# The first norm of the last block: factors applied to sums, gain rows spread by TensorE, and an early half of the second gate products

## The chip, the cores and the metric

The kernel runs as one program on one core of a Trainium2 chip. The metric is device time in microseconds (us) of one execution. TensorE (PE, with its weight loads shown as PEld), VectorE (DVE), ScalarE (ACT), GpSimd (POOL) and SyncE (SP) each have their own instruction stream; instructions of one engine run in order, and engines wait for each other at semaphores. Transfers from memory are issued by SP and POOL here.

## The reference, cut to what matters

A first block of mixers and a routed expert layer is followed by a norm, and that by two layers of a second block, which begins with a norm and a gated feed-forward part. The change sits where the two blocks meet. What is computed there, for 256 tokens of width 1024 in 32-bit floats:

```python
for e in range(32):                                   # two of the 32 experts count for a token
    h = silu(x2d @ w_gate[e]) * (x2d @ w_up[e])       # 1024 -> 256
    y = y + combine[:, e:e + 1] * (h @ w_down[e])     # 256 -> 1024
h = h + y
x = rmsnorm(h, final_norm_g)                          # ends the first block
# second block, layer 0
xn = rms_norm(x, ffn1_norm_2[0])
x = x + 0.5 * (silu(xn @ w_gate) * (xn @ w_up)) @ w_down
```

Both norms divide each token by its root mean square and multiply by a row of gains. So the normed token is its raw sum, times both rows of gains, times one number for the token: the token's factor.

## The kernel before, in words

The 256 tokens are two halves of 128 (j = 0, 1), the 1024 channels two halves of 512 (n = 0, 1). `Moe.run` goes through the experts in eight quads of four (q = 0 to 7); the tokens of an expert, at most 32, stand on 32 partitions of the quad's 128. For each quad:

- `up(a, q, 0)` and `up(a, q, 1)`, L1236: the gate products and the up products, 32 each for the two, `mx<-mw,XG` in the trace (eight blocks of channels by four experts; each half is 32 instructions that the trace may show as two records each, so that a quad has 128);
- `act`, L1403: the message `msg` from silu and the slot weights (ACT, DVE), transposed on TensorE, copied as `mhT` (ACT);
- `down(q, hT)`, L1246: 16 products `mx<-mw,mhT` of 512 columns, the two channel halves in two tiles of their own;
- `back(q, ys, n)`, L1268: each half is cut into a high part (`yh`, ACT) and a low part (`yl`, DVE), which go back to the tokens by products with the one-hot matrix, `acc<-yh,OHT` and `acc<-yl,OHT`, onto the running sums `py[j, n]`. For quad 7's second half the two parts are called `yr`.

Between them other work of the routing is laid: in quad 0, after `down`, the second part of the slot weights (`acc<-cw,OH`, `acc<-mask,ones`), `beyond`, and one of the sums' starts (`acc<-x,ident`); in each quad the gathering of the next quad's tokens. The order on each engine is the program's where `K.ordered` is set; elsewhere a scheduler places instructions.

Weights come through a ring of slots `mw` in SBUF by `load_next`, all issued on SyncE in a fixed order, each when the slot it needs has been read for the last time. `spare(name, slot)` uses a slot of the ring for another tile: the row `fg` of the first norm's gains, for which POOL issues a transfer that repeats the row on all 128 partitions (L1329), and a scratch tile for squares. The second norm's row is `grow`, spread in the same way by `K.gain_row` (L197). `par` are small parameters of later layers, laid out by transposes (L125, L1474) and a product with ones (`mx<-par,ones`) in quad 7.

After quad 7 the norm of the first block and the next one are joined: `gained` multiplies the sums by `fg` (DVE), `square` and `square_x` give the sums of squares before and after the gains (ACT), and a list of one-column steps (`eps`, then `nra`, `nri`, `nrc`) gives each half's factor `rs[j]` (DVE). `Block2.first_part`, L1596, then makes the normed tokens (`norm`: `xn<-x,nri,grow` on DVE, eight transposes), and the first weights of the feed-forward part meet them. Half j = 0 is multiplied whole (`whole(i)`: `acc<-wr,x`, in 32-bit floats, 8 products of 512 columns); half j = 1 and all later work by high and low parts of tokens (`X`) and weights (`wh` on ACT, `wl` on DVE), three products for one (`mm`: `acc<-wh,X`, `acc<-wl,X`, 24 products). From then on the feed-forward part's own loop (`ffn`, L1694) runs: `acc<-X,wh` and `acc<-X,wl` on L246. `unit()` takes the next piece of weights and so also places its `wh` and `wl`.

## Time and profile before

| | us |
|---|---|
| median of 3 runs | 1619.53 (1617.61 to 1621.09) |
| the profiled execution | 1621.05 |
| its span | 1619.4 |
| PE busy in the span | 1548.0 (96%) |
| DVE busy | 1033.5 (64%) |
| ACT busy | 826.9 (51%) |
| POOL busy | 38.8 (2%) |

The profile is of one execution, so its durations add up to 1621.05 us, of which 1.65 lie around the span. A row of the timeline says when an instruction, or a run of like ones (x32), started, how long it took, on which engine and source line, what it wrote and read, and in brackets how long the engine had been idle before it and what ended that. A line such as L48 or L246 is that of a helper that many places call, so one goes by the names of the tiles. The expert stage runs from about 240 to 437 us; the join of the blocks lies between 423 and 461 us; everything after is the second block.

### The profile page before, as it was taken

The numbers are of one execution on the slowest core, as the hardware profiler recorded it, in microseconds if no ns is written. First come the engines' busy times: TensorE is split into PE (matmuls) and PEld (weight loads), VectorE is DVE, ScalarE is ACT, GpSimd is POOL, SyncE is SP. The second block draws the span as 40 slices with busy tenths as digits, with TensorE's granted clock in tenths as the row PEclk, the third lists the DMA queues.
The fourth block names the chain that finished last, engine by engine and source line by source line (L and its number), as shares of the span: only waits on it lengthen the run. The fifth ranks groups of instructions, "written<-read, shape, count | busy, mean of one in ns | idle before, by whom it ended". The sixth has DMA issues, their size and how long they took to land.

```text
span 1619.4 us, 25065 instructions
## 1 busy us (share of the span) xinstructions
PE 1548.0 (96%) x9718; PEld 1279.3 (79%) x9718; DVE 1033.5 (64%) x1913; ACT 826.9 (51%) x1406; POOL 38.8 (2%) x132
## 2 busy tenths in 40 slices
PE   8999998887799999999999999999999999999998
PEld 6989864443378888889878888888888989778887
DVE  6766651111376656868986665666658779876653
ACT  5633421111356544668645654455546677455643
POOL 3000000001000000000000000000000000000000
PEclk9999998999899999999999999999999999999999
DMA  6431599999966656553456655656565534455653
GB/s 201 146 101 66 214 383 395 420 420 418 350 195 185 193 183 193 171 166 98 154 182 197 195 193 182 195 183 192 176 211 187 157 124 153 167 159 186 199 177 112
DMA packets 195644, 331.29 MB, mean 205 GB/s; under 512 B 11972, under 2 KB 150674, under 8 KB 183362
## 3 DMA queue, kind: packets, MB, share of 16 engines
q1 hardware_dynamic: 186208, 315.19, 56.6%
q0 software_dynamic: 4528, 13.41, 2.5%
q8 instruction: 77, 1.26, 0.3%
q10 hardware_dynamic: 4786, 1.05, 0.3%
q14 instruction: 45, 0.37, 0.1%
HBM read 328.25 MB, written 1.38 MB: 204 GB/s over the span
## 4 chain that ended last, share of the span: by engine, by line
PE 70%; DMA 6%; DVE 3%; ACT 2%; issue 1%; ACTq 0%; SPq 0%; DVEq 0%
PE acc L246 40%; PE mx L246 19%; PE acc L48 8%; PE mx L48 3%; DMA mw<-in_exp_w_down 3%; DMA mw<-in_exp_w_up 2%; DMA mw<-in_exp_w_gate 1%; DVE wl L258 1%; DVE wl L48 1%; PE mx L1976 0%; PE mx L2000 0%; ACT fsq L48 0%; ACT wh L277 0%; ACT p L1991 0%; PE mx L2046 0%
## 5 line engine op out<-in xcount | busy, mean ns | idle before, releaser
L258 DVE TENSOR_TENSOR wl<-wr,wh 128x1024 fp32r<-128x1024 f32 x358 | 436.6, 1223 | 269.6 <-ACT wh L277 267.0
L277 ACT ACTIVATE wh<-wr 128x1024 fp32r<-128x1024 f32 x358 | 377.9, 1058 | 365.6 <-PE acc L246 256.7
L246 PE MATMUL acc<-X,wh 128*128 128x256 f32 (+1 forms) x1664 | 357.1, 329 | 0.0
L246 PEld LDWEIGHTS acc<-X,wh 128*128 128x128 f32 x1664 | 277.2, 191 | 25.2 <-issue 4.2
L246 PE MATMUL acc<-X,wl 128*128 128x256 f32 x1152 | 237.2, 285 | 0.0
L246 PEld LDWEIGHTS acc<-X,wl 128*128 128x128 f32 x1152 | 186.4, 191 | 6.9
L246 PE MATMUL mx<-X,wh 128*128 128x512 f32 x640 | 162.0, 393 | 0.0
L246 PEld LDWEIGHTS mx<-X,wh 128*128 128x128 f32 x640 | 114.6, 189 | 19.8
L246 PE MATMUL acc<-wh,hh 128*128 128x512 f32 x288 | 112.2, 390 | 0.0
L246 PE MATMUL acc<-wl,hh 128*128 128x512 f32 x288 | 112.2, 390 | 0.0
L246 PE MATMUL acc<-wh,hl 128*128 128x512 f32 x288 | 112.2, 389 | 0.0
L246 PEld LDWEIGHTS mx<-X,wl 128*128 128x128 f32 x640 | 88.4, 190 | 7.0
L246 PE MATMUL mx<-X,wl 128*128 128x256 f32 x640 | 90.5, 282 | 0.0
L48 PE MATMUL mx<-mw,XG 128*32 128x256 f32 x1024 | 66.3, 403 | 8.0 <-DMA mw<-in_exp_w_up 6.0
L48 PEld LDWEIGHTS mx<-mw,XG 128*32 128x32 f32 x1024 | 34.9, 116 | 37.4 <-issue 9.1
L246 PEld LDWEIGHTS acc<-wh,hl 128*128 128x128 f32 x288 | 54.1, 188 | 11.2
L246 PEld LDWEIGHTS acc<-wl,hh 128*128 128x128 f32 x288 | 54.1, 188 | 11.1
L246 PEld LDWEIGHTS acc<-wh,hh 128*128 128x128 f32 x288 | 54.1, 188 | 11.1
L246 PE MATMUL acc<-wh,m 128*128 128x512 f32 x192 | 61.3, 394 | 0.0
L48 DVE COPY xr<-mx 128x512 f32<-128x512 f32 x8 | 5.5, 691 | 72.7 <-ACT xr L48 72.7
L246 PE MATMUL acc<-xh,wh 128*128 128x256 f32 x176 | 50.4, 286 | 0.0
L246 PE MATMUL acc<-xh,wl 128*128 128x256 f32 x176 | 50.0, 284 | 0.0
(640 smaller groups left out, 2518.7 us busy)
## 6 DMA issues: line engine op xcount, KB each, us to landing
wr<-in_w_in SPq DMA_DIRECT2D x44, 1024.0 KB, 5.4
wr<-in_ffn_w_gate SPq DMA_DIRECT2D x88, 512.0 KB, 4.0
wr<-in_ffn_w_up SPq DMA_DIRECT2D x88, 512.0 KB, 5.0
wr<-in_ffn_w_down SPq DMA_DIRECT2D x40, 1024.0 KB, 5.0
mw<-in_exp_w_gate SPq DMA_DIRECT2D x32, 1024.0 KB, 15.1
mw<-in_exp_w_up SPq DMA_DIRECT2D x32, 1024.0 KB, 16.8
mw<-in_exp_w_down SPq DMA_DIRECT2D x31, 1024.0 KB, 17.9
wr<-in_w_out SPq DMA_DIRECT2D x20, 1024.0 KB, 4.9
```

Of the source, the lines that this page charges most:

```text
L48: return lambda *a, **k: self.tc.keep_in_program_order(f(*a, **k))
L246: self.engines()[2].matmul(out, l, r, start=start, stop=stop, skip_group_check=share)
L258: i = self.K.engines()[0].tensor_sub(l, v, h)
L277: self.K.engines()[1].activation(h, v[:, q:q + c], AF.Copy)
```

## The change

`down` writes both channel halves into one tile of two banks, and `back` reads them from it. The first half of quad 1's products (`up(a, 1, 0)`) is called in quad 0 right after `down`, ahead of the slot weights, and its `load_next` with it. The two rows of gains come as single rows of 4 KB, onto two partitions of one tile, and a new function `every` spreads each with two products of ones (`mx<-fg,ones`) and two copies on ACT; the first is called after `up(a, 7, 1)`, the second after quad 7's parameter steps, and a product of both rows (`both`) is made. For the first half of tokens, `turn` multiplies the sums by `both`, `turned` transposes the result right away, and `whole` runs on tokens without their factor. The factor comes in twice: `act` in `ffn` scales the first gate and up sums by it, and before the tokens are cut into high and low parts, `x0` is multiplied by the factors, spread over the partitions by a product of a diagonal (`dg`) with ones (`pr`). The squares and steps of the second half of tokens come first, those of the first half after it.

```diff
         def down(q, hT):
-            ys = []
+            y = K.mx.tile([P, 2, 512], F32, name="mx")
             for n in range(2):
-                y = K.mx.tile([P, 512], F32, name="mx")
...
+        def every(out, i):
+            b = K.mx.tile([P, 2, 512], F32, name="mx")
+            for n in range(2):
+                K.mm(b[:, n], K.ones[32 * i:32 * i + 1], rows_[i][:, 512 * n:512 * n + 512])
+            V, S, _ = K.engines()
+            for n in range(2):
+                S.activation(out[:, 512 * n:512 * n + 512], b[:, n], AF.Copy)
...
+            order = [(v, j) for v in (yh, yl) for j in range(2)]
+            if q == 7 and n:
+                order.sort(key=lambda o: o[1])
...
+            if q != 1:
+                a = K.mx.tile([P, 1024], F32, name="mx")
+                up(a, q, 0)
+                load_next(4)
+            if q == 7:
+                fg = spare("fg", 12, n=2048)
+                rows_ = [fg[32 * i:32 * i + 1, D:] for i in range(2)]
+                for i, src in enumerate((A["final_norm_g"], A["ffn1_norm_2"][0])):
+                    nc.gpsimd.dma_start(rows_[i], bass.AP(tensor=src.tensor, offset=src.offset, ap=[[0, 1], [1, D]]))
+                fg = fg[:, :D]
+            up(a, q, 1)
             load_next(4)
             if q == 7:
-                fg = spare("fg", 11)
-                src = A["final_norm_g"]
-                nc.gpsimd.dma_start(fg, bass.AP(tensor=src.tensor, offset=src.offset, ap=[[0, P], [1, D]]))
-            up(a, q, 1)
-            load_next(4)
+                every(fg, 0)
...
             if q == 7 and B:
                 next(par, None)
+                B.given = K.xp.tile([P, D], F32, name="grow")
+                every(B.given, 1)
+                both = spare("both", 13)
+                K.V.tensor_mul(both, fg, B.given)
             y = down(q, hT)
             load_next(4)
             if q == 0:
+                a = K.mx.tile([P, 1024], F32, name="mx")
+                up(a, 1, 0)
+                load_next(4)
                 slot_weights(1, 8)
...
+        def turn(n):
+            V.tensor_mul(x0[:, half[n]], py[0, n], both[:, half[n]])
+        def turned(n):
+            pt.append(K.mx.tile([P, 4, P], F32, name="mx"))
+            for k in range(4):
+                K.T.transpose(pt[n][:, k], x0[:, (4 * n + k) * P:(4 * n + k + 1) * P], K.ident)
+        back(7, y, 1)
+        turn(0)
         gained(0, 0)
-        back(7, y, 1)
...
+        turn(1)
+        turned(0)
+        turned(1)
+        square(0, 0, sq)
+        square(1, 0, sq)
+        for j, n in ((1, 0), (1, 1), (0, 1)):
+            gained(j, n)
...
# Block2.first_part
+        for k4, p in zip(k4s, pt):
+            S.activation(x0[:, k4], p, AF.Copy)
+        square(1, 1, fsq)
+        for n in range(2):
+            square_x(1, n, fsq)
         unit()
         whole(0)
+        run(es[1])
+        next(norm)
...
+        square(0, 1, fsq)
+        for n in range(2):
+            square_x(0, n, fsq)
         unit()
         whole(3)
+        next(norm)
+        run(es[0])
         self.stream.ahead = AHEAD
-        self.mm(1, us)
-        for k0 in range(0, KD, 4):
-            self.parts(0, slice(k0, k0 + 4), x0[:, k0:k0 + 4])
+        dg = pool.tile([P, P], F32, name="dg", tag="hl")
+        V.tensor_scalar(dg, K.ident, rs[0], None, op0=OP.mult)
+        self.mm(1, us[:2])
+        pr = K.mx.tile([P, P], F32, name="mx")
+        K.mm(pr, K.ones, dg)
+        for k4 in k4s:
+            V.tensor_mul(x0[:, k4], x0[:, k4], pr[:, None].to_broadcast([P, 4, P]))
+            self.parts(0, k4, x0[:, k4])
+        self.mm(1, us[2:])
```

TensorE in quad 0, from its down products to quad 1's; `XG_2524` and `XG_2525` are quad 1's gathered tokens, `cw` the combine weights. Before:

```order
L48 MATMUL mx<-mw,mhT 32x512 x16
L48 MATMUL acc<-cw,OH_2276 128x5 x7
L48 MATMUL acc<-cw,OH_2277 128x5 x7
L48 MATMUL acc<-mask,ones 128x32 x2
L48 MATMUL acc<-x,ident 128x512
L48 MATMUL acc<-yh,OHT 128x512 x2
```

After the change, TensorE at the same place:

```order
L48 MATMUL mx<-mw,mhT 32x512 x16
L48 MATMUL mx<-mw,XG_2524 32x256 x16
L48 MATMUL mx<-mw,XG_2525 32x256 x16
L48 MATMUL acc<-cw,OH_2276 128x5 x7
L48 MATMUL acc<-cw,OH_2277 128x5 x7
L48 MATMUL acc<-mask,ones 128x32 x2
```

The first 32 of quad 1's 64 gate and up products moved ahead of the slot weights and of quad 0's `back`.

TensorE in quad 7, up to its down products; `XG_3634` and `XG_3635` (after: `XG_3628`, `XG_3629`) are its tokens. Before:

```order
L48 MATMUL mx<-mw,XG_3634 32x256
L125 MATMUL mx<-ident,par 128x120
L125 MATMUL mx<-ident,par 128x86
L48 MATMUL mx<-mw,XG_3634 32x256
L48 MATMUL mx<-par,ones 128x512
L48 MATMUL mx<-par,ones 128x32
L1474 MATMUL mx<-ident,par 128x2
L48 MATMUL mx<-mw,XG_3634 32x256 x14
L48 MATMUL mx<-mw,XG_3635 32x256 x16
L48 MATMUL mx<-mw,XG_3634 32x256 x16
L48 MATMUL mx<-mw,XG_3635 32x256 x16
L48 MATMUL mx<-ident,msg 128x128 x2
```

After the change, TensorE from the last up products of quad 7 on:

```order
L48 MATMUL mx<-mw,XG_3629 32x256 x16
L48 MATMUL mx<-fg,ones 128x512 x2
L125 MATMUL mx<-ident,par 128x120
L125 MATMUL mx<-ident,par 128x86
L48 MATMUL mx<-ident,msg 128x128 x2
L48 MATMUL mx<-par,ones 128x512
L48 MATMUL mx<-par,ones 128x32
L1507 MATMUL mx<-ident,par 128x2
L48 MATMUL mx<-fg,ones 128x512 x2
L48 MATMUL mx<-mw,mhT 32x512 x16
```

The parameter products moved from among the gate products to between the last up product and `down`, and the rows' products stand with them.

DVE from the norm products of the second half of tokens to the low parts of its transposed tokens. Before:

```order
L48 SCALAR_TENSOR_TENSOR xn<-x,nri,grow 128x512 x2
L48 TENSOR_TENSOR wl<-wr,wh 128x1024
L48 TENSOR_TENSOR X<-mx,X 128x4x128 x2
L48 TENSOR_TENSOR wl<-wr,wh 128x1024
L48 TENSOR_TENSOR X<-x_3884,X 128x4x128 x2
```

After the change, DVE at the same place, followed by the first of the other half's one-column steps:

```order
L48 SCALAR_TENSOR_TENSOR xn<-x,nri,grow 128x512 x2
L48 TENSOR_TENSOR wl<-wr,wh 128x1024 x3
L48 TENSOR_TENSOR X<-mx,X 128x4x128 x2
L48 TENSOR_SCALAR rse<-fst 128x1
L48 SCALAR_TENSOR_TENSOR fa<-fst,rse 128x1
```

Three low parts of weights in place of one now stand ahead of the tokens' low parts, and the first of the four stands ahead of the second half's own one-column steps.

## Rows read from the trace of the kernel before

**Rows 1.** The page's part 4: the chain that ended last, by engine, by line

```profile
PE 70%; DMA 6%; DVE 3%; ACT 2%; issue 1%; ACTq 0%; SPq 0%; DVEq 0%
PE acc L246 40%; PE mx L246 19%; PE acc L48 8%; PE mx L48 3%; DMA mw<-in_exp_w_down 3%; DMA mw<-in_exp_w_up 2%; DMA mw<-in_exp_w_gate 1%; DVE wl L258 1%; DVE wl L48 1%; PE mx L1976 0%; PE mx L2000 0%; ACT fsq L48 0%; ACT wh L277 0%; ACT p L1991 0%; PE mx L2046 0%
```

**Rows 2.** Windows; busy us by engine, then granted clock, DMA share, GB/s

```profile
270.00:272.00 2.00, 2.00 (x44) 1.23 (x40) 0.00 (x0) 0.00 (x0) 0.00 (x0) 1.00 0.23 90
272.00:274.00 2.00, 2.00 (x44) 1.18 (x37) 0.00 (x0) 0.00 (x0) 0.00 (x0) 1.00 0.75 188
...
350.00:380.00 30.00, 26.93 (x250) 12.48 (x254) 5.80 (x10) 6.40 (x16) 0.00 (x0) 1.00 1.01 420
```

**Rows 3.** Timeline of SyncE's queue (start us, duration us, what it issues)

```profile
271.42 0.80 SPq L1058 DMA_DIRECT2D mw<-in_exp_w_down  x2
```

**Rows 4.** Timeline of PE: quad 1's gate and up products

```profile
267.75 7.11 PE L48 MATMUL mx<-mw,XG 128*32 128x256 f32 x128
```

**Rows 5.** Timeline of PE: quad 7, last up and first down products

```profile
423.00 3.64 PE L48 MATMUL mx<-mw,XG 128*32 128x256 f32 x58 [0.28 <-DMA mw<-in_exp_w_up]
...
428.70 1.60 PE L48 MATMUL mx<-mw,mhT 128*32 128x512 f32 x4 [0.47 <-ACT mhT L48]
```

**Rows 6.** Timeline of PE: from quad 7 to the feed-forward loop

```profile
444.50 1.94 PE L48 MATMUL mx<-ident,xn 128*128 128x128 f32 x8 [5.54 <-DVE xn L48]
...
454.73 0.80 PE L48 MATMUL acc<-wh,X 128*128 128x512 f32 x1
...
460.58 1.52 PE L246 MATMUL acc<-X,wh 128*128 128x512 f32 x6
```

**Rows 7.** Timeline of POOL: the two broadcasts of gain rows

```profile
383.33 0.55 POOL L1329 DMA_DIRECT2D fg<-in_final_norm_g  x1 [207.92 <-PE mx L48]
...
419.96 0.58 POOL L197 DMA_DIRECT2D grow<-in_ffn_norm  x1 [10.42 <-ACT big L1489]
```

**Rows 8.** Timeline of PE: the parameter steps in quad 7

```profile
414.04 1.26 PE L48 MATMUL mx<-par,ones 1*128 1x512 f32 x4
...
416.84 0.19 PE L1474 MATMUL mx<-ident,par 2*128 2x2 f32 x1 [1.54 <-DVE par L48]
```

**Rows 9.** Timeline of ACT: second eviction of quad 7, a high part

```profile
436.85 0.60 ACT L1274 ACTIVATE yr<-mx 128x512 fp32r<-128x512 f32 x1 [1.06 <-PE mx L48]
...
443.48 1.04 ACT L48 ACTIVATE wh<-wr 128x1024 fp32r<-128x1024 f32 x1
```

**Rows 10.** Timeline of PE: an earlier quad whose weights were there

```profile
350.62 0.51 PE L48 MATMUL mx<-ident,msg 128*128 128x128 f32 x2 [1.80 <-DVE msg L48]
...
351.96 3.95 PE L48 MATMUL mx<-mw,mhT 128*32 128x512 f32 x32
```

**Rows 11.** Timeline of DVE: gains, one-column steps, norm products, low parts

```profile
438.09 2.49 DVE L48 TENSOR_TENSOR x<-acc,fg 128x512 f32<-128x512 f32 x4
...
442.05 0.15 DVE L48 TENSOR_SCALAR nri<-nri 128x1 int32<-128x1 int32 x1
...
443.00 0.16 DVE L48 SCALAR_TENSOR_TENSOR nri<-nrc,nri 128x1 f32<-128x1 f32 x1
443.60 1.41 DVE L48 SCALAR_TENSOR_TENSOR xn<-x,nri,grow 128x512 f32<-128x512 f32 x2 [0.44 <-ACT fsq L48]
...
445.61 1.23 DVE L48 TENSOR_TENSOR wl<-wr,wh 128x1024 fp32r<-128x1024 f32 x1
...
453.80 1.29 DVE L48 TENSOR_TENSOR X<-mx,X 128x512 fp32r<-128x512 f32 x2 [1.28 <-ACT X L48]
```

**Rows 12.** Timeline of PE: quad 0's message, after a wait

```profile
250.71 0.70 PE L48 MATMUL mx<-ident,msg 128*128 128x128 f32 x2 [3.05 <-DVE msg L48]
```

**Rows 13.** Windows after three waits of PE; columns as in Rows 2

```profile
250.60:253.60 3.00, 2.90 (x14) 2.21 (x18) 0.50 (x2) 0.38 (x1) 0.00 (x0) 0.50 1.01 426
...
350.60:353.60 3.00, 2.98 (x26) 1.63 (x26) 0.69 (x1) 1.19 (x5) 0.00 (x0) 1.00 1.02 423
...
444.50:448.00 3.50, 3.50 (x10) 2.37 (x11) 2.82 (x10) 2.14 (x5) 0.00 (x0) 0.50 0.00 0
```

More of the change, by code (lines that the diff above doesn't have):

```diff
@@ L1598, in first_part @@
         K = self.K
-        rs, ra, rest, last = first
-        grow = self.grow
+        rs, ra, es, last, pt, square, square_x = first
         self.begin(part)
         K.ordered = True
+        V, S, _ = K.engines()
         units, us = self.first_units(part), []
@@ L1608, in first_part @@
         x0 = pool.tile([P, KD, P], F32, name="x0", tag="hh")
-        norms = [self.norm(x, j, grow, pool, "xn", rs[j], w) for j, w in ((0, x0), (1, None))]
+        fsq = pool.tile([P, 512], F32, name="fsq", tag="hl")
+        norm = self.norm(x, 1, self.grow, pool, "xn", rs[1])
+        k4s = [slice(k0, k0 + 4) for k0 in range(0, KD, 4)]
         def whole(i):
@@ L1714, in put @@
             nc.vector.tensor_sub(hl[:, f], h, hh[:, f])
-        h0 = [act(a[:, 0:256], a[:, 256:512], 256) for a in ac]
+        h0 = [act(a[:, 0:256], a[:, 256:512], 256, first[0][0] if first and j == 0 else None) for j, a in enumerate(ac)]
         def sums(i):
```

73 lines of the change are left out of this document (29 added, 44 removed).

## The prediction

> **What bounds the kernel now.** The first look is at the chain of waits: TensorE's own work is 70% of it, transfers 6%, and the transfers in it are expert weights [rows 1]. So there are two kinds of time to win: TensorE's standing still, and, in the expert stage, whatever delays the stream of weights. The second look is the table of windows by DMA rate: the stream runs at 420 GB/s while it is limited by itself, but falls to 90 and 188 GB/s from 270 to 274 us [rows 2]. SyncE's queue says why: the loads that come next were issued at 271.42 us and later, when their slots came free [rows 3], and the slots are freed by the up products of quad 1, which TensorE began at 267.75 us [rows 4]. The third look is the end of the expert stage: the last up weights let TensorE go on at 423.00 us [rows 5], so a byte less, or an idle stretch less, in the stream moves that moment. From there to the last block's steady rhythm at 460.58 us [rows 6] the path is a string of short steps on three engines, in which TensorE stood still for 5.54 us before the first transposes [rows 6]. After 460.58 us products follow each other without a hole, in both kernels in the same order; what happens before that moment is the whole question.
>
> **Earlier weights (a gain).** The hole in the stream: two microseconds at 90 and two at 188 instead of 420 GB/s are 2 x (1 - 90/420) + 2 x (1 - 188/420) = 1.57 + 1.10 = 2.7 us. The change puts half of quad 1's up products (half of the 7.11 us of [rows 4], 3.55 us) ahead of quad 0's remaining work (slot weights, back), so the slots come free some 10 us earlier and the hole should close. TensorE's sum of work there is the same; what was late is only late by what was moved ahead of it, and it ends where it did. The two norm rows: each was a broadcast of 128 x 4 KB = 0.52 MB, issued at 383.33 and 419.96 us [rows 7], in a stretch at 420 GB/s: 1.25 us of the stream each. Now 4 KB each. The second was issued 3 us before the last up weights came; I count a third of it, 0.4 us (ends 0 and 1.25). Sum: 2.7 + 1.25 + 0.4 = **4.3 us** earlier. The up products of quad 7, which ended at 423.00 + 3.64 = 426.64 us [rows 5], then end at 422.3.
>
> **Quad 7 between up and down (a loss).** Before, 2.06 us lay between the end of up and the start of down at 428.70 [rows 5], and the parameter work for later layers stood among up products that waited for weights anyway, so it cost nothing: its product with ones at 414.04, its last transpose at 416.84 [rows 8]. In the new order all of it stands behind the 64 up products and ahead of down, together with the rows' products. Step by step: two products of ones with a 512-wide row: such a product together with a 32-wide one took 1.26 [rows 8], so about 0.85 each, 1.7; two ACT copies of 128x512 at 0.60 [rows 9], 1.2, for which the parameter transposes wait, since they need the tile that these free; the message's chain without its last copy, about 1.4 of the 2.06 us; from the parameter's ones product to its last transpose 416.84 - 414.04 = 2.8, and 0.2 for the transpose; two more row products, 1.7. That is 9.0; some of it can lie side by side (parameter transposes beside the message's ACT step), so I take **8.5 us**. Then the 16 down products (32 records), all weights there: 3.95 us, as in an undisturbed quad [rows 10]. Down ends at 422.3 + 8.5 + 4.0 = **434.8** us, against 436.8 before (the second eviction started at 436.85 [rows 9]). Of 4.3 us won, 2.0 are left. Bounds: the chain is hidden wholly (5.2 us left, the down weights gaining both rows in full) or costs the full 9.0 (1.5 left).
>
> **From the end of down to the steady rhythm (a loss).** Before: 460.58 - 436.85 = 23.7 us [rows 6, 9]. After, ACT's first eviction waits for the last down product, since both halves are one tile; the path is ACT's and DVE's, not TensorE's. Eviction, low part, eviction, low part: 4 steps of 0.60 to 0.65, 2.5. A new product with both gains for the first tokens, then the plain one: 2 of DVE's 2.49 / 4 = 0.62 [rows 11], 1.24. Two squares on ACT, of the eviction's width and time (0.60 [rows 9]): 1.2; two gains 1.24; three squares 1.8; the raw weights' high part 1.04 [rows 9] and low part 1.23 [rows 11], which the new order puts ahead of the factor's small steps; twelve of those at (443.00 - 442.05) / 5 = 0.19 [rows 11], 2.3; two norm products 1.41; three more low parts 3.7; the low part of the transposed tokens 0.65 (half of 1.29) [rows 11]. Together 18.3, and about 0.9 for a dozen hand-overs and the squares' accumulator reads: 19.2. TensorE's whole products of the first tokens, which now need no factor, start early and are done by then: they are off the path. Then the second low part 0.65, ten small steps 1.9, one low part of the next weights 1.2, two small steps 0.3, another low part 1.2 and the diagonal 0.2 come before the product that spreads the factors, and behind that 12 of the 24 split products, half of the 5.85 us from 454.73 to 460.58 [rows 6], 2.9. That is 8.3; the first of these overlaps what runs, so 8.0. Sum 19.2 + 8.0 = **27.2 us**, 3.5 more than before. The steady rhythm starts at 434.8 + 27.2 = 462.0 instead of 460.6: **+1.4 us**.
>
> **The clock.** TensorE waits twice there: for the transposed tokens' low part, since DVE's three weight parts and this one take 3.7 + 0.65 while the transposes and a copy take about 1.7, some 2.6 us; and for the factors, since DVE's steps up to the diagonal take 5.4 us and the first 12 split products 2.9, some 2.5 to 3 us. In the trace the transposes after 3.05 us without work ran with the clock at 0.50, 1.2 GHz instead of 2.4 (0.70 us for two) [rows 12, 13], those after 1.80 us at 1.00 (0.51 us for two) [rows 10, 13]; after 5.54 us again at 0.50 [rows 6, 13], as the window from 444.50 us shows. The two new waits lie between. If both bring the half clock, the second 12 products cost 2.9 more and the first some tenths; if neither, nothing; one more thing on the other side, the half clock at 444 to 448, is no longer on the path and is in the sum already. I take **+1.0**, with 0 and 3.0 as ends. The Trainium skill, TensorE: Matmul & The Clock Gate, Part 1 (What's actually happening), says that throttled is the default and activity releases it; by that each of the new waits is a danger, and the sum would be the first rival's. The 1.80 us rows speak against reading it for every short wait.
>
> **Other edits.** The step back of each other quad gets about 0.7 us longer, because the second half's eviction waits for the first half's low part; in those quads TensorE waits for weights, so it is hidden (if not: 0.7 for each quad in which the weights are early, of which only the first two could be such). Scaling the gate sums within the activation and one fused product in place of a plain one: the same instructions; nothing. ACT's table load ahead of the first scaled activation falls where ACT has room.
>
> **Sum.** 1.4 + 1.0 = +2.4 us on the profiled run of 1621.05 us, whose span is 1619.4; it lies 1.5 above the median of 1619.53. The same step on the median gives **1621.9 us**. What this measurement can tell from no change is about 0.2%, 3.2 us; the forecast is within it. Its own range, from the bounds of the second row's third, the overlap and the clock, is 1619.5 to 1622.7, where the clock rival takes over.
>
> **Rivals.** *Slower, by the clock:* both new waits end with TensorE at 1.2 GHz. 1.4 + 3.0 = +4.4, 1623.9 us. It decides if the half clock costs over 1.8 us on the path. For it: the row after 3.05 us. Against: the rows after 1.80 us. *Slower, the hole stays:* the change does not do what it says, because the early up products themselves wait (for quad 1's last weights, or the gathered tokens), and the loads are issued as late as before. Then 2.7 of the 4.3 us are missing: 2.4 + 2.7 = +5.1, 1624.6 us. *Faster:* the string between up and down in quad 7 lies beside work, because transposes and products with ones overlap more than their rows show, and down is bound by weights 5.2 us earlier: 436.8 - 5.2 + 27.2 = 458.8, -1.8 us; and the first tokens' early sums shorten the string behind it to what it was, 23.7: -5.3, 1614.3 us. It needs most of both. For it: the first tokens' norm products and factor no longer stand ahead of TensorE's first products, where it waited 5.54 us; against: DVE's order, which puts four low parts between the squares and the split products.
>
> **Chances.** Forecast and what lies near it 0.50; clock rival 0.17; hole rival 0.13; other slips beyond +3.2 us 0.02; faster 0.18. So faster 0.18, same 0.50, slower 0.32. The range for 8 in 10 reaches to most of the rivals on each side: 1615.5 to 1625.5 us.
>
> **What the profile will show.** Right: no window from 268 to 276 under 400 GB/s; loads issued near 261; the last up products of quad 7 ending near 422; some 8 us to down's start; split products in two groups of 12 with holes of 2 to 3 us ahead of each; the steady rhythm near 462. Wrong: down starting within 4 us of up's end, or the rhythm starting before 459 (faster), or after 464 (slower). A change in the time after the rhythm has started, at the same order of products, would be a step that this working does not have.

## Result, and the profile after

| | before | after |
|---|---|---|
| median, us | 1618.74 (4 runs, 1617.61 to 1621.09) | 1630.46 (4 runs, 1626.52 to 1631.15) |
| ratio to before | | 1.0069, 95% interval 1.0055 to 1.0083 |
| the profiled execution, us | 1621.05, span 1619.4 | 1626.52, span 1624.9 |

The change makes the kernel slower by 0.69%, 11.7 us by the medians. The forecast of 1621.9 was wrong, and so was its range.

The two profiles can't be laid over each other from the start of the span. After's profiled run is the fastest of its four, and before's lies above its median. A good part of this is settled before the change begins: quad 0's message, ahead of which nothing is changed, stood at 250.71 us in before [rows 12] and at 246.67 in after. That it comes early is no effect of the change, for it came at 247.01 and 246.84 us in two experiments whose quad 0 is that of before (e10_fillonly and e2_first). So below I count from this message. TensorE in after (start us, duration us, engine, line, output and inputs, count, and the wait ahead with what ended it):

```profile
246.67 0.70 PE L48 MATMUL mx<-ident,msg 128*128 128x128 f32 x2 [3.06 <-DVE msg L48]
...
254.30 3.63 PE L48 MATMUL mx<-mw,XG 128*32 128x256 f32 x64
...
267.62 3.66 PE L48 MATMUL mx<-mw,XG 128*32 128x256 f32 x64
...
415.79 5.69 PE L48 MATMUL mx<-mw,XG 128*32 128x256 f32 x58 [1.43 <-DMA mw<-in_exp_w_up]
421.42 1.98 PE L48 MATMUL mx<-fg,ones 1*128 1x512 f32 x4
424.57 0.32 PE L125 MATMUL mx<-ident,par 120*128 120x120 f32 x1 [1.18 <-ACT fg L48]
...
426.10 1.67 PE L48 MATMUL mx<-par,ones 1*128 1x512 f32 x4
429.31 0.23 PE L1507 MATMUL mx<-ident,par 2*128 2x2 f32 x1 [1.54 <-DVE par L48]
429.31 3.77 PE L48 MATMUL mx<-fg,ones 1*128 1x512 f32 x4
433.02 5.62 PE L48 MATMUL mx<-mw,mhT 128*32 128x512 f32 x32
...
457.45 1.18 PE L48 MATMUL acc<-wh,X 128*128 128x512 f32 x2 [2.53 <-DVE X L48]
...
464.29 0.71 PE L48 MATMUL mx<-dg,ones 128*128 128x128 f32 x2 [2.69 <-DVE dg L48]
...
468.94 1.53 PE L246 MATMUL acc<-X,wh 128*128 128x512 f32 x6
```

Quad 1's first half now stands at 254.30 us, 13 us ahead of its second half. The last up weights of quad 7 let TensorE go on 415.79 - 246.67 = 169.1 us after the message, against 423.00 - 250.71 = 172.3 before [rows 5, 12]: 3.2 us won. Then everything is longer than it was reckoned: the last up products took 5.69 instead of 3.64 us; 11.5 us lie between up's end (421.48) and down's start (433.02); and the same pair of products of ones with a row took 1.98 us at 421.42 and 3.77 us at 429.31. The windows say why (columns as in [rows 2]; the granted clock is third from the right):

```profile
415.00:420.00 5.00, 4.21 (x40) 1.98 (x44) 0.00 (x0) 0.00 (x0) 0.00 (x0) 0.50 1.00 416
420.00:425.00 5.00, 3.72 (x27) 1.38 (x19) 0.07 (x1) 1.45 (x3) 0.00 (x0) 1.00 1.04 373
425.00:430.00 5.00, 3.10 (x9) 1.80 (x10) 2.69 (x11) 3.10 (x4) 0.00 (x0) 0.68 1.08 343
430.00:435.00 5.00, 5.00 (x16) 1.25 (x18) 2.02 (x8) 1.78 (x6) 0.00 (x0) 0.50 0.47 151
```

TensorE ran at 0.50, 1.2 GHz, until 420 us, for most of the last up products, and again from 427 to 437 us, through the second row product and most of `down`. The kernel before had a stretch of half clock in quad 7 too, but earlier. Windows of before:

```profile
418.00:419.00 1.00, 1.00 (x16) 0.51 (x12) 0.69 (x4) 0.18 (x2) 0.00 (x0) 0.50 1.00 418
...
422.00:423.00 1.00, 0.72 (x10) 0.13 (x2) 0.00 (x0) 0.00 (x0) 0.00 (x0) 1.00 1.00 418
```

And of after:

```profile
412.00:413.00 1.00, 0.00 (x0) 0.00 (x0) 0.00 (x0) 0.00 (x0) 0.00 (x0) 1.00 1.02 426
...
414.00:415.00 1.00, 0.36 (x1) 0.00 (x0) 0.00 (x0) 0.00 (x0) 0.00 (x0) 0.50 0.98 410
```

Before, the parameter steps and their waits stood among the gate products. The clock was at 0.50 from about 417.6 to 421 us, in 66 records of products that took 5.76 us and ended 0.28 us before the last up weights came, and it was back at 1.00 for these. In after the like 66 records took 4.07 us and ended at 410.29. Then TensorE stood still for 3.8 of the 5.5 us until 415.79, waiting for weights, and the clock fell at about 413.2 us, ahead of the last up products.

The rhythm of the feed-forward loop begins at 468.94 us, 222.3 after the message; before it was 460.58 - 250.71 = 209.9 [rows 6, 12]. These 12.4 us are of the size of the 11.7 of the medians; the two profiled executions differ by only 5.5, since after's reached the message 4.0 us earlier and needed 2.9 less behind the rhythm. Behind that point the span goes on for 1156.0 us in after and 1158.8 in before; in all sixteen profiles of this study it is between 1155.6 and 1159.8, with no relation to the edit. So what happens between the message and the rhythm is the whole matter, as the forecast had it.

The hole in the stream is closed. Windows of after:

```profile
268.00:270.00 2.00, 2.00 (x44) 1.17 (x36) 0.00 (x0) 0.00 (x0) 0.00 (x0) 1.00 1.03 426
270.00:272.00 2.00, 2.00 (x26) 1.01 (x19) 0.00 (x0) 0.00 (x0) 0.00 (x0) 1.00 1.00 414
272.00:274.00 2.00, 2.00 (x6) 0.88 (x5) 0.00 (x0) 0.00 (x0) 0.00 (x0) 1.00 1.01 422
```

In before SyncE issued two loads of down weights from 257.96 us on and the next two at 271.42 [rows 3], with nothing from 259.7 on between them. In after all four were issued by 258.75 us:

```profile
255.39 3.36 SPq L1058 DMA_DIRECT2D mw<-in_exp_w_down  x4
```

Two loads of gate weights followed by 259.9 us. The queue stood still here too, until 271.29 us, but with four loads of 1 MB more on their way.

And DVE in after, ahead of the two waits of the first part (same columns as TensorE's timeline):

```profile
453.31 3.49 DVE L48 TENSOR_TENSOR wl<-wr,wh 128x1024 fp32r<-128x1024 f32 x3
456.71 1.28 DVE L48 TENSOR_TENSOR X<-mx,X 128x512 fp32r<-128x512 f32 x2
...
463.87 0.28 DVE L48 TENSOR_SCALAR dg<-ident,nri 128x128 f32<-128x128 f32 x1
```

Three low parts of weights, 3.49 us, stand ahead of the tokens' low part for which TensorE waits 2.53 us, and the diagonal comes last of a long row of steps; TensorE waits 2.69 us for it.

### The profile page after: what moved, and what is told of

The parts are those of the page before. It is cut to its first block, busy times and chain, and to the rows that moved or that the text cites. A ratio compares the mean times of both kernels' runs of the same rounds, so it can differ in the third digit from the quotient of the medians.

```text
span 1624.9 us, 25093 instructions
## 1 busy us (share of the span) xinstructions
PE 1549.5 (95%) x9728; PEld 1277.0 (79%) x9728; DVE 1036.5 (64%) x1917; ACT 829.4 (51%) x1410; POOL 38.8 (2%) x132
## 3 DMA queue, kind: packets, MB, share of 16 engines
q8 instruction: 77, 1.26, 0.3%
## 4 chain that ended last, share of the span: by engine, by line
PE 69%; DMA 7%; DVE 3%; ACT 2%; issue 1%; POOL 0%; SPq 0%; ACTq 0%; DVEq 0%
PE acc L246 39%; PE mx L246 18%; PE acc L48 7%; PE mx L48 4%; DMA mw<-in_exp_w_up 3%; DMA mw<-in_exp_w_down 1%; DMA mw<-in_exp_w_gate 1%; DMA cr<-csd 1%; DVE wl L258 1%; DVE wl L48 1%; PE mx L2027 0%; ACT wh L277 0%; PE mx L2051 0%; ACT p L2042 0%; PE mx L2097 0%
## 5 line engine op out<-in xcount | busy, mean ns | idle before, releaser
L246 PE MATMUL acc<-xl,wh 128*128 128x256 f32 x176 | 50.5, 287 | 0.0
```

Of the source, the lines that this page charges most:

```text
L246: self.engines()[2].matmul(out, l, r, start=start, stop=stop, skip_group_check=share)
```

## The experiments

The table takes each profile apart at two points: from quad 0's message to the end of `down` in quad 7 (the end of the last record of `mx<-mw,mhT`), and from there to the rhythm. In before this end is 436.81 us:

```profile
433.19 3.62 PE L48 MATMUL mx<-mw,mhT 128*32 128x512 f32 x26 [0.32 <-DMA mw<-in_exp_w_down]
```

The fourth column is the difference of the two together from before's 209.9; the last one is measured independently, over all runs of the kernel, against before on the same chip.

| kernel | message to down's end | down's end to rhythm | sum against before | ratio, 95% interval |
|---|---|---|---|---|
| before | 186.1 | 23.8 | | |
| after | 192.0 | 30.3 | +12.4 | 1.0069 (1.0055 to 1.0083) |
| e1_quad1 | 183.8 | 25.6 | -0.5 | 0.9996 (0.9986 to 1.0006) |
| e2_first | 188.5 | 27.5 | +6.1 | 1.0033 (1.0021 to 1.0046) |
| e3_q7early | 185.4 | 30.2 | +5.7 | 1.0036 (1.0022 to 1.0049) |
| e4_warm | 195.0 | 27.4 | +12.6 | 1.0082 (1.0068 to 1.0097) |
| e5_rowsdma | 183.1 | 29.2 | +2.4 | 1.0022 (1.0011 to 1.0033) |
| e6_nofirst | 193.4 | 24.7 | +8.2 | 1.0050 (1.0036 to 1.0064) |
| e7_fill | 183.1 | 23.7 | -3.1 | 0.9987 (0.9976 to 0.9997) |
| e8_warm2 | 192.1 | 27.4 | +9.7 | 1.0049 (1.0033 to 1.0066) |
| e9_fullrows | 190.3 | 28.8 | +9.2 | 1.0057 (1.0038 to 1.0075) |
| e10_fillonly | 186.3 | 22.3 | -1.2 | 0.9977 (0.9967 to 0.9987) |
| e11_order | 183.2 | 24.8 | -1.9 | 0.9972 (0.9962 to 0.9983) |
| e12_orderfill | 183.3 | 25.1 | -1.4 | 0.9992 (0.9980 to 1.0003) |
| e13_parearly | 189.7 | 30.3 | +10.1 | 1.0043 (1.0030 to 1.0057) |
| e14_parlate | 186.6 | 33.4 | +10.1 | 1.0044 (1.0031 to 1.0057) |

0.0010 of the ratio is 1.6 us. The two last columns agree within 3.2 us everywhere, less than the spread of the time behind the rhythm (4.2 us); each profile is one execution.

**One part at a time.** Two parts of the change alone, and then its parts left out. First the early half of quad 1 with `down`'s one tile, on the kernel before:

```diff
+            y = K.mx.tile([P, 2, 512], F32, name="mx")     # down
...
+            if q != 1:
+                a = K.mx.tile([P, 1024], F32, name="mx")
+                up(a, q, 0)
+                load_next(4)
...
             if q == 0:
+                a = K.mx.tile([P, 1024], F32, name="mx")
+                up(a, 1, 0)
+                load_next(4)
                 slot_weights(1, 8)
```

> The kernel before with two pieces of the change alone: down writes one tile, and the first half of quad 1's products stands in quad 0 behind down. If the early loads are worth what they were counted at, the hole of 2.7 us in the weight stream closes, the last up weights come 2.7 us earlier, and of it the later eviction of quad 7's first half takes back some 0.7 us: 2.0 us (0.12%) faster than before. If this piece is itself harmful (quad 0's return step late, evictions longer in each quad), it is slower than before by up to 5 us.

The last up products began 417.20 - 247.14 = 170.1 us after the message, 2.2 earlier than in before, and `down` ended 2.3 earlier. But 1.9 of these were lost again behind it, and the time is that of before. By its interval the early half alone gives 0.14% at most.

The first part alone on the kernel before (factors on sums, the new order of steps), with rows by transfers and the old quad loop (shown against after, and cut):

```diff
-                fg = spare("fg", 12, n=2048)
...
+                fg = spare("fg", 11)
+                nc.gpsimd.dma_start(fg, bass.AP(..., ap=[[0, P], [1, D]]))
...
-                every(B.given, 1)
+                B.given = K.gain_row(A["ffn1_norm_2"][0])
```

> The kernel before with the new first part of the last block alone (first tokens without factor, factor on the sums; rows of gains still broadcast by transfers, parameters among quad 7's products). If the first part is what costs: from the end of quad 7's down to the steady rhythm about 27 us instead of 23.7 at full clock, so +3 us, and +6 us if both new waits bring 1.2 GHz. If the new order between up and down of quad 7 is what costs, the time stays within 2 us of before.

TensorE in e2_first:

```profile
427.54 0.70 PE L48 MATMUL mx<-ident,msg 128*128 128x128 f32 x2 [4.61 <-DVE msg L48]
...
442.01 10.00 PE L48 MATMUL acc<-wr,x 128*128 128x512 f32 x16 [2.78 <-ACT x L48]
...
454.42 0.74 PE L48 MATMUL acc<-wh,X 128*128 128x512 f32 x2 [0.54 <-DVE X L48]
```

From down's end to the rhythm it takes 27.5 us, where the prediction has 27.2 without the clock. The clock was not at 1.00 throughout: it was at 0.50 from 441 to 447.8 us, and the whole products took 10.00 us, where they took 7.13 in after. But TensorE still waited for the low part behind them, 0.54 us here and 2.53 in after, so this half clock was not what set the length. The wait of 4.61 us is the edit's own: `both` stands ahead of the message's step on DVE and waits for the transfer of `grow`. It costs 2.2 us at down's end (188.5 against 186.3 in e10_fillonly, whose quad 7 is that of before), so the first part alone is worth some 3 to 4 us of loss.

After with broadcast rows, so that nothing new stands between up and down (the parameter steps go back among the gate products of quad 7):

```diff
-                fg = spare("fg", 12, n=2048)
...
+                fg = spare("fg", 12)
+                nc.gpsimd.dma_start(fg, bass.AP(..., ap=[[0, P], [1, D]]))
-                every(fg, 0)
...
-                every(B.given, 1)
+                B.given = K.gain_row(A["ffn1_norm_2"][0])
...                                       # `both` is made behind the last down, ahead of back(7, y, 1)
```

> The changed kernel with the two rows broadcast by transfers again, as before; so the parameter steps of quad 7 fall back among its gate products, and one tile for down, the early half of quad 1 and the new first part stay. If the string between up and down (11.5 us in the changed kernel) is most of the loss, it is 2.1 here, the last weights come some 2 us later (1 MB more), and the kernel is 5 to 7 us faster than the changed one, +4 to +6 on before, which is the first part's own cost. If it is all the first part, it is as slow as the changed kernel, +10 or more.

TensorE in e5_rowsdma:

```profile
418.93 3.64 PE L48 MATMUL mx<-mw,XG 128*32 128x256 f32 x58 [1.59 <-DMA mw<-in_exp_w_up]
...
428.96 3.62 PE L48 MATMUL mx<-mw,mhT 128*32 128x512 f32 x26 [0.32 <-DMA mw<-in_exp_w_down]
```

Up and down are at the full clock, and down ends 8.9 us earlier from the message than in after (183.1 against 192.0). The kernel is still slower than before, by 0.22%, through the first part.

And the opposite: after with before's first part, so with the early half and all that lies between up and down:

```diff
 # before, with e1's edit, the rows as in after, and
+                every(fg, 0)
...
                 next(par, None)
+                B.given = K.xp.tile([P, D], F32, name="grow")
+                every(B.given, 1)
...
-        self.grow = K.gain_row(g)
+        self.grow, self.given = self.given or K.gain_row(g), None
```

> The changed kernel with the first part of before: one tile, the early half and the rows spread by TensorE in quad 7, with the parameter steps behind up, stay. If string and first part add up, this one costs what the changed kernel has over the first part's +5: about +5 to +6 on before, with 10 to 12 us between up and down. If the first part is all, within 2 us of before.

The string took 11.4 us (up's end 422.68, down 434.11), its second row product 3.78 us and `down` 5.72, with the clock at 0.50; behind it 24.7 us. The parts add up: e5_rowsdma (early half and first part) +0.22%, e6_nofirst (early half and string) +0.50%, less the early half that both have (e1_quad1, -0.04%): 0.76%, against the change's 0.69%. Two thirds of the loss come with the string between up and down and the half clock in the products on both sides of it (in e6_nofirst the last up products too took 5.80 us), one third with the first part.

**Where the half clock falls.** Rows and parameters of quad 7 ahead of its second half of products, the up products, in after:

```diff
                 fg = fg[:, :D]
+                every(fg, 0)
+                next(par, None)
...
+                every(B.given, 1)
...
             up(a, q, 1)
...
-                every(fg, 0)
...
-                next(par, None)
-                every(B.given, 1)
```

> The changed kernel, with rows and parameter steps of quad 7 moved ahead of its second half of products (the up products), where TensorE waits for weights. If the string between up and down is the main cost, 11.5 us there shrink to 2 to 3, down then ends when its weights are there, and the kernel is 6 to 8 us faster than the changed one: +3 to +5 us on before. If the first part or the early half of quad 1 is the main cost, it gains under 3 us.

TensorE in e3_q7early:

```profile
420.23 3.78 PE L48 MATMUL mx<-fg,ones 1*128 1x512 f32 x4 [0.25 <-DVE par L1506]
423.94 5.19 PE L48 MATMUL mx<-mw,XG 128*32 128x256 f32 x64
...
431.24 3.64 PE L48 MATMUL mx<-mw,mhT 128*32 128x512 f32 x32 [0.47 <-ACT mhT L48]
```

The half clock moved with the steps: now the row product and the up products have it, and `down` took 3.64 us. Down's end came 6.6 us earlier than in after (185.4 against 192.0), and the kernel is 0.33% faster than after by the two ratios. The work is the same; standing where TensorE waits for weights anyway it costs 2.3 us to down's end (185.4 against 183.1 in e5_rowsdma, which has neither string nor single rows), instead of 8.9.

Next, products that add nothing, of zeros on running sums, in the five waits (two in the string, three in the first part), first 64 by 64, then the full 128 by 128:

```diff
+                K.fill(py[0, 0], 4)       # behind every(fg, 0)
...
+        K.fill(self.py, 7)                # behind mx<-par,ones; 6 in e8_warm2
...
+        K.fill(self.ac[1], 5, True)       # ahead of the transposes
...
+                    K.fill(self.ac[j], fill)   # in both waits of the split products, 10
```

> The changed kernel with products by a matrix of zeros (they add nothing) at five places where TensorE waits: after the first row's products, after the parameters' product with ones, ahead of the second half's transposes, ahead of the low part, ahead of the factors' product. Each lasts at full clock about as long as the wait. If the half clock is the main cost, the granted clock stays at 1.00 from 421 to 469 us, the second row's products take 1.8 instead of 3.8 us, down 3.7 instead of 5.6, the split products 2.9 for 12 instead of 4.2: 5 to 7 us faster than the changed kernel. If the cost is the length of the chains at any clock, the time is that of the changed kernel or up to 1 us more.

> The changed kernel with products of a full 128x128 matrix of ones with zeros (they add nothing) in the same five waits, in place of the 64x64 ones tried before, and a little fewer in the parameters' wait. If the half clock in quad 7's string comes from how little TensorE works there and can be held off so, the clock is 1.00 from 421 on, the second row's products take 1.8 us and down 3.7, and the kernel is 5 to 7 us faster than the changed one. If the products of one row and of 32 columns themselves leave the clock at half, the string is as slow as in the changed kernel or slower, and only the waits of the first part gain 2.9 us.

TensorE in e8_warm2:

```profile
428.90 2.52 PE L48 MATMUL acc<-zero,ones 128*128 128x512 f32 x4
...
431.35 3.78 PE L48 MATMUL mx<-fg,ones 1*128 1x512 f32 x4
435.05 5.87 PE L48 MATMUL mx<-mw,mhT 128*32 128x512 f32 x32
...
468.34 1.66 PE L254 MATMUL acc<-X,wh 128*128 128x512 f32 x6 [0.95 <-DVE X L48]
```

Its windows:

```profile
430.00:435.00 5.00, 5.00 (x8) 1.50 (x6) 1.99 (x11) 1.88 (x5) 0.00 (x0) 0.50 0.70 227
...
460.00:465.00 5.00, 5.00 (x21) 3.50 (x21) 3.94 (x16) 2.37 (x3) 0.00 (x0) 1.00 1.03 352
```

In the first part both kinds of products kept the clock at 1.00, and both kernels took 27.4 us from down's end to the rhythm, against 30.3 in after: the clock costs 2.9 us there, and what is left is the prediction's 27.2. (The rhythm then waits for DVE's low part `X`, 0.95 us in e8_warm2.) In the string both failed: the clock fell all the same, with TensorE busy for the whole of 430 to 435 us. In e4_warm the products only made the string longer (`down` began at 437.08, 14 us behind the end of up), which is why that kernel is slower than after.

Row products over all 128 partitions (the row with zeros around it, against a column of the identity):

```diff
+                nc.gpsimd.memset(fg[:, D:], 0.0)
...
-                K.mm(b[:, n], K.ones[32 * i:32 * i + 1], rows_[i][:, 512 * n:512 * n + 512])
+                K.mm(b[:, n], K.ident[:, 32 * i:32 * i + 1].to_broadcast([P, P]), wide[:, 512 * n:512 * n + 512])
```

> The changed kernel with the rows spread by products over all 128 partitions (the other 126 hold zeros, put there by GpSimd ahead of the rows' transfers) in place of products of a single row. If it is the single-row products that leave TensorE's clock at half in quad 7's string, the clock stays at 1.00 from 421 on, the second row's products take 1.8 instead of 3.8 us and down 3.7 instead of 5.6: 4 us faster than the changed kernel. If it is the waits of the string as such, nothing changes beyond 1 us.

TensorE in e9_fullrows:

```profile
419.21 1.98 PE L48 MATMUL mx<-fg,ident 128*128 128x512 f32 x4
...
426.87 3.78 PE L48 MATMUL mx<-fg,ident 128*128 128x512 f32 x4
430.58 4.44 PE L48 MATMUL mx<-mw,mhT 128*32 128x512 f32 x32
```

The same two durations, so it is not that a product reads a single row. `down` took 4.44 us here instead of 5.62, with the clock back at 1.00 from 432.2 us on; what brought it back sooner the run doesn't tell.

Last, one of the two contents of the string at a time: the rows alone, with the parameter steps among the gate products, and the parameters alone, with rows by transfers.

```diff
 # e13_parearly: after, and
                 fg = fg[:, :D]
+                next(par, None)
             up(a, q, 1)
...
-                next(par, None)
 # e14_parlate: e5_rowsdma, with the parameters' transposes kept in their written place
-        nc.tensor.transpose(pt, rows, self.ident[:n, :n])
+        self.engines()[2].transpose(pt, rows, self.ident[:n, :n])
```

> The changed kernel with the parameter steps of quad 7 back among its gate products; the rows by TensorE stay between its up and its down projection. The changed kernel has 11.5 us between the two projections, of which about 2.2 are half clock. Theory (the sum of the parts counts, wherever the clock falls): between up and down stand then the first row product 2.0, its wait 1.2, the message 0.5 and the second row product 2.0, at the full clock 5.5 to 6.5 us, so 4 to 5 us less than in the changed kernel and 6 to 8 us more than in the kernel before; down takes 3.64 at full clock. Rival (the row products themselves bring the half clock): the second row product takes 3.78 and down 5.6 again, and the kernel is only 1 to 2 us faster than the changed one.

> The changed kernel with the norm rows spread by transfers as before, but the parameter steps of quad 7 held between its up and its down projection. Theory (the waits for the other engines on the parameters are what lengthens the stretch): between up and down stand the message's 2.1 and the parameters' 1.3 with their wait of 1.5, some 5 to 6 us, about 3 us more than the same kernel with parameters among the gate products (e5_rowsdma), so about 6 us over the kernel before; down at the full clock, 3.64. Rival (the parameters and their waits bring the half clock): down takes 5.6, and the kernel comes within 1 to 2 us of the changed one.

TensorE in e13_parearly:

```profile
423.06 1.98 PE L48 MATMUL mx<-fg,ones 1*128 1x512 f32 x4
428.51 0.70 PE L48 MATMUL mx<-ident,msg 128*128 128x128 f32 x2 [3.47 <-DVE msg L48]
429.14 3.78 PE L48 MATMUL mx<-fg,ones 1*128 1x512 f32 x4
432.85 6.12 PE L48 MATMUL mx<-mw,mhT 128*32 128x512 f32 x32
```

And in e14_parlate:

```profile
418.76 5.21 PE L48 MATMUL mx<-mw,XG 128*32 128x256 f32 x58 [1.42 <-DMA mw<-in_exp_w_up]
...
429.16 5.13 PE L48 MATMUL mx<-mw,mhT 128*32 128x512 f32 x32
...
440.56 1.65 PE L48 MATMUL acc<-yr,OHT 128*128 128x512 f32 x3 [3.63 <-DVE yr L48]
```

With the rows alone the string is still 9.8 us long (423.06 to 432.85), where the theory had 5.5 to 6.5: 2.0 of it are half clock, and the wait for the message is 3.47 us, where the theory had a wait of 1.2, since both copies of the row and a table load of 1.28 us stand ahead of the message's step on ACT. The sum by the ratios, 0.26% less than after, is what the theory gave, but not for its reason: from message to rhythm it is 2.3 us, not 4 to 5. With the parameters alone the string is 5.2 us (423.97 to 429.16), as expected, and the clock at 0.50 from 428.8 to 432.2 us takes 1.5 more in `down`. So neither content is the culprit by itself; each brings waits and then the half clock into a stretch of the path that had none. The 3.63 us are again the edit's own: `both` waits on DVE for the transfer of `grow`.

**The clock outside the change.** Before, TensorE stood still for 5.54 us ahead of the first transposes and went on at half clock [rows 6, 13]. Six products of constants that nobody reads, put into this wait, on e1_quad1 and on the kernel before:

```diff
         back(7, y, 1)
...
+        b = K.mx.tile([P, 512], F32, name="mx")
+        for _ in range(6):
+            K.mm(b.rearrange("p (a b) -> p a b", a=4), K.ones, K.ident[:, None].to_broadcast([P, 4, P]))
...
         square(1, 0)
```

> The kernel before with one tile, the early half of quad 1, and six products of constants into a tile that nobody reads, put where TensorE waits 5.5 us behind quad 7. If the clock is what the wait costs, the granted clock stays 1.00 from 439 to 448 us, transposes take 1.05 instead of 1.94 us and the whole products lose their slow start: 1.9 us faster than without them, 3 us (0.2%) faster than before. If not, no difference to before and to the version without them.

> The kernel before with nothing but six products of constants in the wait of 5.5 us behind quad 7. By the clock theory the transposes (1.94) and whole products behind the wait run at 2.4 GHz: 1.8 to 2.0 us faster than before (0.12%). If the gain of 3 us that was seen together with the early half of quad 1 came mostly from that half, under 1 us.

TensorE in e10_fillonly:

```profile
435.31 5.31 PE L48 MATMUL mx<-ident,ones 128*128 128x512 f32 x12
441.02 1.29 PE L48 MATMUL mx<-ident,xn 128*128 128x128 f32 x8 [0.40 <-DVE xn L48]
```

The clock stayed at 1.00 in both from 435 us on; the transposes took 1.29 instead of 1.94 us [rows 6]. From down's end to the rhythm it is 22.3 against 23.8 us in the one, 23.7 against 25.6 (e1_quad1) in the other. Before with these six products is 0.23% faster than before, and no change lies outside its interval. That is 3.7 us by the ratio, of which the profile shows 1.4 in this stretch; the rest is not accounted for.

**The order on DVE.** e5_rowsdma, with the squares and steps of the first half and the diagonal ahead of the second half's tokens, and three of the weights' low parts behind them:

```diff
+        late = self.stream.late = []       # the low parts of the next four weights are kept
...
         next(norm)
+        run(late[:1])
         square(0, 1, fsq)
...
         run(es[0])
         V.tensor_scalar(dg, K.ident, rs[0], None, op0=OP.mult)
+        next(norm)                         # the other half's high and low parts
+        run(late[1:])
```

> The version with rows by transfers (changed kernel otherwise, +3 to +4 us on before), with another order of DVE's work in the first part: the first half's squares and one-column steps and the diagonal ahead of the transposed tokens' low part, and the three low parts of weights behind it. If the first part is slow because DVE's three weight parts stand ahead of the tokens' low part and the factor's steps behind it, the two waits of 2.5 and 2.8 us go, the steady rhythm starts some 24 us after quad 7's down instead of 29, and it is 3 to 5 us faster than that version: 0 to -1 us on before. If the first tokens' early sums are slow for another reason, within 1 us of that version.

TensorE in e11_order:

```profile
448.50 0.50 PE L48 MATMUL acc<-wh,X 128*128 128x512 f32 x1 [2.62 <-ACT X L48]
...
453.20 0.38 PE L48 MATMUL mx<-dg,ones 128*128 128x128 f32 x2
```

Its DVE:

```profile
447.43 0.28 DVE L48 TENSOR_SCALAR dg<-ident,nri 128x128 f32<-128x128 f32 x1
...
448.48 1.29 DVE L48 TENSOR_TENSOR X<-mx,X 128x512 fp32r<-128x512 f32 x2
449.68 3.49 DVE L48 TENSOR_TENSOR wl<-wr,wh 128x1024 fp32r<-128x1024 f32 x3
```

The diagonal is ready 5.5 us before TensorE asks for it, the second wait is gone, and one of 2.62 us is left. Down's end to rhythm is 24.8 instead of 29.2 us. The kernel is 0.28% faster than before and 0.96% faster than after: factors on the sums cost nothing by themselves (24.8 us against 25.6 in e1_quad1, which has before's first part); the order of DVE's steps did. The size is less sure than the direction: against e5_rowsdma it is 4.3 us by the profiles and 0.50%, 8 us, by the ratios. With products of constants in the remaining wait as well:

```diff
         next(norm)
+        for i in range(3):
+            K.mm(a[:, :m], K.ones, K.ident[:, None].to_broadcast([P, m, P]), i == 0, False, True)
         run(late[1:])
```

> The version with the other order on DVE, and three products of constants in the one wait of 2.6 us that it has left, ahead of the split products (into a sum that is started anew behind them). If that wait's half clock is still on the path, the first 12 split products take 2.9 instead of 4.5 us, the steady rhythm starts 1 to 1.5 us earlier after quad 7's down (23.5 us in place of 24.8), and it is 1 us faster than without: -0.3 to -0.4% on before. If DVE's work sets the rhythm's start by then, no gain.

The clock was at 1.00 throughout, but the rhythm began no sooner (25.1 us behind down's end): TensorE waited 1.11 us for DVE's low part `X` there. TensorE's clock was no longer what ended last, and by the ratios the kernel is no faster than e11_order, but 0.20% slower (the two intervals just overlap), with nearly the same sum of parts (-1.4 and -1.9 us).

## Why the prediction was wrong, step by step

| step, us | predicted | measured | too little by |
|---|---|---|---|
| last up weights, from the message, against before | -4.3 | -3.2 | 1.1 |
| last up products | 3.64 | 5.69 | 2.0 |
| between up and down | 8.5 | 11.5 | 3.0 |
| down | 3.95 | 5.62 | 1.7 |
| down's end to the rhythm, with 1.0 for the clock | 28.2 | 30.3 | 2.1 |
| sum against before | +2.4 | +12.4 | 10.0 |

- **Earlier weights:** right in mechanism, 1.1 us less than reckoned. The hole closed; the loads that stood at 271.42 us in before were issued by 259.9 us. From the message to the last up weights it took 172.3 to 172.5 us in the three kernels without the early half (before, e2, e10), 169.8 on the mean in the six that have it and broadcast rows (e1, e5, e7, e11, e12, e14), 168.7 in five with single rows (after, e4, e6, e8, e9). So the hole was worth 2.6 us (reckoned: 2.7) and, by these means, the rows 1.1 (reckoned: 1.65), though single runs of the two kinds overlap (169.4 to 171.1 and 167.7 to 170.4); after's own run lies 0.4 above the mean of its kind.
- **Between up and down:** the list of steps was right, and its sum at the full clock nearly: 11.5 less 1.8 for the second row product (3.77 against 1.98) and 0.4 for the parameters' product (1.67 against 1.26 [rows 8]) is 9.3, against 8.5 and a bound of 9.0. The row products were a term that was too small, 1.98 instead of 1.7 for each pair.
- **The clock, the step that failed.** The prediction asked what the clock does at the two waits of the first part and took 1.0 us for it, from rows after short waits. It did not ask the same of the stretch that it had itself just filled with waits, between up and down: up, the string and down were priced at rows of the full clock. What the runs showed in its place: there the half clock took 2.0 us in the up products, 2.2 in the string and 1.7 in `down`. In the first part it took 2.9 (30.3 against 27.4 in e4_warm and e8_warm2), nearly the upper end of 3.0. Together 8.8 us, where 1.0 stood: 7.8 of the 10.0 missing. The clock rival had the mechanism, but its price of 3.0 was for the first part alone. Nor do the runs bear out what the prediction read from its rows, half clock after a wait of 3.05 us and full clock after 1.80. In after the clock fell in the string at about 426.8 us, behind waits of 1.18 and 0.38 us, and after the same wait of 3.06 us in quad 0 three other runs still had the full clock (last section).
- **From down's end to the rhythm:** right. 27.2 was predicted without the clock; 27.4, 27.4 and 27.5 were measured in e4_warm, e8_warm2 and e2_first (in the last with a half clock that did not set the length). Both waits are there, 2.53 and 2.69 us, for the two reasons given.
- **The rivals:** the hole did not stay; nothing overlapped as the faster one needed, the string lay on the path in full. **Other edits:** no term of the time behind the rhythm showed up.

The Trainium skill, TensorE: Matmul & The Clock Gate, Part 1 (What's actually happening), says that throttled is the default and activity releases it, which the prediction weighed for the two new waits alone. By that rule each stretch with waits is a danger; the trace agrees, at 0.50 in the string, in up and behind both waits of the first part. But work did not release it everywhere: in e4_warm TensorE was busy without a gap from 427.3 to 442 us, and the clock stayed at 0.50.

What stays open is what decides over the clock in the string. Products in its waits, narrow or full, and row products over all partitions did not keep it up; e13_parearly and e14_parlate lost it with either content. In after, e4_warm, e6_nofirst, e8_warm2, e9_fullrows and e14_parlate, where the parameter steps are gone from among the gate products, the last 58 up products took 5.2 to 6.6 us; in before and in e1, e2, e5, e7, e10, e11 and e12, where they stand there, 3.64 each time. In the first six TensorE stood still for 3.8 to 5.1 us in three waits for weights ahead of these products, in the others for 0.3 to 1.8 us. e13_parearly, which differs from after only by the parameter steps back among the gate products, had no such wait, and the clock was at 1.00 from 418 us to the end of up. e14_parlate, which differs from e5_rowsdma only by these steps behind up, shows the reverse: 5.21 against 3.64 us. So the place of the parameter steps decides over the half clock in up; that it does so by the waits fits all the runs, but was not tested by itself. A version with the string at the full clock was not found.

## What to carry to other kernels

Work that is moved out of a stretch which waits for weights into one that doesn't has to be priced twice: by its own steps, and by the clock that its waits leave for TensorE behind them, here 5.9 us for up, string and down against 0.8 for the steps that were mis-sized. When a factor is taken off the path, look at the order of the engine that makes it: here another order of the same steps on VectorE took 4.4 us off the path, and a kernel 0.22% slower than before became 0.28% faster. And count from an event ahead of the change, not from the start of the span, before two profiles are compared.

## What the runs showed of the hardware that was not expected

- TensorE can be busy without a gap and stay at 1.2 GHz for long: in e4_warm from 430 to 440 us the granted clock was 0.50 with TensorE busy for all of both windows of 5 us, through products of 64 by 64, rows and `down`'s 128 by 32. In the same run it fell to 0.50 between 425 and 426 us, when TensorE had been busy without a gap, by the profile, since 416.68.
- The same wait does not always bring the same clock. Ahead of quad 0's message TensorE waited 3.05 or 3.06 us in all sixteen profiles. The two transposes behind it took 0.50 or 0.51 us, at 1.00, in e6_nofirst, e10_fillonly and e13_parearly, and 0.65 to 0.70 in the others, with the clock at 0.50 or falling in them.
- Full products of constants held 2.4 GHz through a wait of some 5 us (5.54 in before and 4.84 in e1_quad1; e10_fillonly, e7_fill), and products of zeros, 64 by 64 or full, held it through the shorter waits of the first part (e4_warm, e8_warm2).
- A pair of row products takes 1.98 us at 1.00 and 3.78 at 0.50, whether they read one partition or 128 (after, e9_fullrows).
- A load of an activation table takes 1.28 us on ACT, and moving the parameter steps moved one of them onto the path in e13_parearly (426.16 to 427.44 us, the message's step at 427.46). The Trainium skill, ScalarE: Activation LUTs, What ACT_TABLE_LOAD costs, gives about 1283 ns for the load by itself; the trace agrees.
